# A decoder step on one core: TensorE's side work as single products between the big products, in place of runs at the start of a block

## The chip, the cores and the metric

One core of one Trainium2 chip runs the whole kernel. The metric is device time in microseconds (us): the median of three runs. "Product" below means one matrix product or one transpose issued to TensorE (PE in the profile). A product of plain fp32 operands shows as two matmul instructions in the profile, a transpose and an fp32r product as one.

## The reference, cut to what matters

One layer of a hybrid decoder, on 256 prompt rows and 8 x 4 sample rows, all in fp32:

```
proj = x @ w_in                                   # 2048 -> 11280 columns
gB, gC, h, q, k, v, z, b, a, m_a, m_b = split(proj)
y_a  = (gB * conv3(gC * h)) @ w_a_out
q, k, v = silu(conv4(q|k|v)); q, k l2-normalised; beta = sigmoid(b); g = -exp(a_log) * softplus(a + dt_bias)
# per head, per chunk of 64 rows:
M = strict_lower(beta k k^T * decay);  T = inverse(I + M)
u = T (v beta);  w = T (k beta exp(gcum));  attn = q k^T * decay
v_new = u - w S;  o = q' S + attn v_new;  S = S * exp(g_last) + k'^T v_new
y_b  = (gated RMSNorm(o) * silu(z)) @ w_b_out
x = LN(ALPHA x + (sig(m_a) y_a + sig(m_b) y_b) @ w_o)
x = LN(ALPHA x + relu(x @ w_up)^2 @ w_down)
```

The outputs are y for prompt and sample, and the new conv and delta-rule states.

## The kernel before, in words

**Big products.** Every weight matrix is cut into blocks of 512 KB: 4 slices of 128 rows by 256 columns. 496 blocks are worked off in one list. A weight is split into a high part (ScalarE, `split_hi`, L179) and a low part (VectorE, `split_lo`, L186 by the helper of L140), both fp32r, and so are the activations. `matmuls(i)` issues 24 products for block i: for each 128 x 128 weight tile high x high, high x low, low x high (L206 to L208), each with 288 moving columns (290 in the up projection), accumulated in a PSUM tile `acc`. These 11,904 products are called big products here.

**The order.** The main loop (L1371) writes the program by hand, block after block: `split_hi(i + 3)`, one step of the side work, `split_lo(i + 3)`, the evacuations of `acc` that are due in this block (`due`, L1397), `matmuls(i)`, and the load of block i + 7. Each engine executes its own instructions in just this order; between engines there are semaphores. Four raw, high and low weight buffers rotate, so `split_hi(i + 3)` waits until block i - 1 has been multiplied.

**Side work** is all else that TensorE does, and what ScalarE, VectorE and GpSimd do with it. It is written as generators. `side()` runs `gates()` and then `gdn(G)` for two groups of four heads; a `yield` ends a step, and the main loop takes one step per block. `aux` holds a second generator, `sample()` of the current group or `states()`, with one step per block too. So all products of a step stand as one run ahead of block i's big products, and the step's other instructions follow the run at once. The products that matter below:

- L1030 and L1031: k k^T and q k^T for four chunks of four heads. Stationary 128 x 64, moving 64 columns, results on PSUM partitions 0 to 63 or 64 to 127 by the parity of the head. 32 products, one run per G.
- `pairs` (L1080, products on L1084): block inverse by doubling, for s = 8, 16, 32, two calls each. Eight pairs of 64 x 64 products, one on the lower and one on the upper half of the rows and columns. Six calls per G.
- `states_of` (products on L1072): initial states of the sample rows. Stationary 128 x 64, moving 128 columns, 16 products in a run; two calls per G, each right behind a `pairs` run.
- L1251: state update k'^T v_new, contraction over 64 rows, four products per chunk, four chunks per G; then L1254, two products over the full array.
- Products and transposes over the full array: L958, L973, L980, L1219 (transposes of k, q, v), L1139 to L1142, L1157, L1165, L1172, L1176, L1183 (sample rows), L1203 (sample state), L1231, L1243 (recurrence), L1291, L1298, L1316, and L608 and L628 in the last phase.

`fill` (L159) is a separate list for the first three blocks: x's 16 tiles are transposed by `x_tile(k)`, three transposes each (the third, L799, over 32 rows only), one tile behind each three big products. `hist_tiles()` transposes nine small tiles ahead of block 4. `gtile()` gives the PSUM tiles for side work, four in rotation.

## Time and profile before

| | before |
|---|---|
| median of three runs (lowest, highest) | 1706.18 us (1704.86, 1707.64) |
| span of the profiled execution | 1703.4 us |
| TensorE matmul busy | 1688.5 us, 13,063 instructions |
| VectorE, ScalarE, GpSimd busy | 1007.2, 734.1, 133.8 us |
| first big product starts, last one ends (us from the span's start) | 9.44, 1688.2 |
| side work between them | 90 runs, 1,105 matmul instructions |

The profile gives the profiled execution's time only as its span, 1703.4 us, which is 2.8 us under the median of the runs. In rows of the timeline the columns are start (us), length (us), engine, source line, operation, tile written <- tiles read, rows x columns of the stationary tile, shape of the moving operand, number of instructions merged. A matmul's length runs to the modelled end of its pipeline, so lengths of neighbours overlap; what a product costs is read from the starts. In rows of the stretches the columns are the stretch, its length, busy us and instruction count of PE, PE's weight loads, DVE, ACT and POOL, then the granted clock, the DMA share and GB/s.

### The profile page before, as it was taken

What the parts mean: (1) busy time and instruction counts of PE and PEld (TensorE: products, weight loads), DVE (VectorE), ACT (ScalarE), POOL (GpSimd) and SP (SyncE); (2) the same over time, 40 slices, a digit from 0 to 9 for tenths busy, and PEclk for the clock granted to TensorE, in tenths of its full rate; (3) what the DMA queues carried; (4) which work ended last, traced back from release to release, by engine and by line L of the source; (5) the groups of instructions that cost most, each with busy time, mean ns of one, the idle gap of its engine ahead of it and who ended that gap; (6) DMA issues with size and microseconds to landing.
All of it is one profiled execution on the core that took longest, in us unless ns stands there. A gap on an engine that the chain in (4) does not pass through costs nothing.

```text
span 1703.4 us, 31106 instructions
## 1 busy us (share of the span) xinstructions
PE 1688.5 (99%) x13063; PEld 1668.7 (98%) x13063; DVE 1007.2 (59%) x1296; ACT 734.1 (43%) x1067; POOL 133.8 (8%) x223
## 2 busy tenths in 40 slices
PE   9999999999999999999999999999999999999997
PEld 7999999999999999999999999999999999999997
DVE  5577876758544444456778844566445654466565
ACT  4675626333543333334445533444334433344442
POOL 2232412023300000000010000000000000000000
PEclk9999999999999999999999999999999999999999
DMA  8464456435555555555565555555555555555552
GB/s 244 140 194 139 123 175 200 150 115 180 162 170 169 166 162 170 163 164 165 158 190 174 165 170 161 164 170 162 167 168 161 163 171 162 164 167 164 162 162 80
DMA packets 275097, 279.18 MB, mean 164 GB/s; under 512 B 13131, under 2 KB 270092, under 8 KB 274952
## 3 DMA queue, kind: packets, MB, share of 16 engines
q1 hardware_dynamic: 270414, 265.95, 51.3%
q0 software_dynamic: 4256, 11.12, 2.3%
q8 instruction: 102, 1.67, 0.4%
q14 instruction: 37, 0.30, 0.1%
q10 hardware_dynamic: 288, 0.13, 0.0%
HBM read 269.68 MB, written 7.48 MB: 163 GB/s over the span
## 4 chain that ended last, share of the span: by engine, by line
PE 98%; DVE 1%; DMA 0%; POOL 0%; issue 0%; SPq 0%; ACT 0%; POOLq 0%; ACTq 0%
PE acc L206 31%; PE acc L208 31%; PE acc L207 31%; PE g L1084 1%; DMA xr<-in_x_prompt_dram 0%; PE g L1072 0%; PE g L1231 0%; PE g L1251 0%; PE g L831 0%; DVE w L143 0%; PE g L1254 0%; PE g L1203 0%; PE g L1243 0%; PE g L608 0%; PE g L798 0%; PE g L958 0%
## 5 line engine op out<-in xcount | busy, mean ns | idle before, releaser
L140 DVE TENSOR_TENSOR lo<-raw,hi 128x1024 fp32r<-128x1024 f32 (+2 forms) x502 | 614.0, 1226 | 556.2 <-ACT hi L179 553.7
L179 ACT CAST hi<-raw 128x1024 fp32r<-128x1024 f32 (+1 forms) x498 | 517.6, 1041 | 765.0 <-PE acc L207 707.7
L206 PE MATMUL acc<-xh,hi 128*128 128x288 f32 x1408 | 422.9, 300 | 0.0
L208 PE MATMUL acc<-xh,lo 128*128 128x288 f32 x1408 | 416.7, 296 | 0.0
L207 PE MATMUL acc<-xl,hi 128*128 128x288 f32 x1408 | 416.5, 296 | 0.0
L206 PE MATMUL acc<-dh,hi 128*128 128x290 f32 x1024 | 303.9, 297 | 0.0
L207 PE MATMUL acc<-dl,hi 128*128 128x290 f32 x1024 | 303.3, 296 | 0.0
L208 PE MATMUL acc<-dh,lo 128*128 128x290 f32 x1024 | 302.7, 296 | 0.0
L206 PE MATMUL acc<-hh,hi 128*128 128x288 f32 x1024 | 302.3, 295 | 0.0
L208 PE MATMUL acc<-hh,lo 128*128 128x288 f32 x1024 | 302.3, 295 | 0.0
L207 PE MATMUL acc<-hl,hi 128*128 128x288 f32 x1024 | 302.3, 295 | 0.0
L206 PEld LDWEIGHTS acc<-xh,hi 128*128 128x128 f32 x1408 | 265.4, 189 | 2.6 <-issue 0.7
L207 PEld LDWEIGHTS acc<-xl,hi 128*128 128x128 f32 x1408 | 265.8, 189 | 0.5
L208 PEld LDWEIGHTS acc<-xh,lo 128*128 128x128 f32 x1408 | 265.6, 189 | 0.0
L206 PEld LDWEIGHTS acc<-dh,hi 128*128 128x128 f32 x1024 | 193.6, 189 | 0.1
L208 PEld LDWEIGHTS acc<-dh,lo 128*128 128x128 f32 x1024 | 193.3, 189 | 0.0
L207 PEld LDWEIGHTS acc<-dl,hi 128*128 128x128 f32 x1024 | 193.3, 189 | 0.1
L207 PEld LDWEIGHTS acc<-hl,hi 128*128 128x128 f32 x1024 | 192.5, 188 | 0.0
L208 PEld LDWEIGHTS acc<-hh,lo 128*128 128x128 f32 x1024 | 192.3, 188 | 0.0
L206 PEld LDWEIGHTS acc<-hh,hi 128*128 128x128 f32 x1024 | 192.1, 188 | 0.0
L207 PE MATMUL acc<-ml,hi 128*128 128x288 f32 x256 | 75.6, 295 | 0.0
L208 PE MATMUL acc<-mh,lo 128*128 128x288 f32 x256 | 75.6, 295 | 0.0
(404 smaller groups left out, 1620.0 us busy)
## 6 DMA issues: line engine op xcount, KB each, us to landing
raw<-in_w_in_dram SPq DMA_DIRECT2D x176, 512.0 KB, 3.5
raw<-in_w_up_dram SPq DMA_DIRECT2D x128, 512.0 KB, 3.9
raw<-in_w_down_dram SPq DMA_DIRECT2D x128, 512.0 KB, 3.7
raw<-in_w_o_dram SPq DMA_DIRECT2D x32, 512.0 KB, 3.7
raw<-in_w_a_out_dram SPq DMA_DIRECT2D x16, 512.0 KB, 3.7
raw<-in_w_b_out_dram SPq DMA_DIRECT2D x16, 512.0 KB, 3.6
S<-in_state_gdn_dram POOLq DMA_DIRECT2D x8, 512.0 KB, 7.8
out_dram<-S POOLq DMA_DIRECT2D x8, 512.0 KB, 4.9
```

The source lines that it names most:

```text
L140: dve.tensor_tensor(out=out, in0=a, in1=b, op=op)
L179: act.copy(his[i][:, k:k + step], raw[i][:, k:k + step])
L206: pe.matmul(o, wh, xh_, start=st, stop=False)
L207: pe.matmul(o, wh, xl_, start=False, stop=False)
L208: pe.matmul(o, wl, xh_, start=False, stop=en)
L1084: pe.matmul(out[r, q * 64:q * 64 + 64], a[r, q, :], b[r, q, :], start=True, stop=True)
```

## The change

`fill` is replaced by a list `live` of generators. `slot()` advances the first of them to its next `yield 1`, that is by one product (or one pair), and is called behind every single big product; what is still left at the end of a block is run out there. The side generators get a `yield 1` behind each product, so a step still takes one block but its products stand one behind each big product; its first product still stands ahead of the block. An ordinary `yield` still ends the step. `steps()` takes one step of `sgen` and one of `aux`, product by product. Since a step is now written while `matmuls(i)` is, its ScalarE and VectorE instructions stand behind `split_lo(i + 3)` and the evacuations of block i, no longer ahead of them. In the k k^T part the loops are turned round, so that a pair on both parities is one unit.

```diff
-    fill = []
+    live = []
+
+    def slot():
+        while live:
+            if next(live[0], None):
+                return
+            live.pop(0)
...
                 pe.matmul(o, wh, xh_, start=st, stop=False)
+                slot()
                 pe.matmul(o, wh, xl_, start=False, stop=False)
+                slot()
                 pe.matmul(o, wl, xh_, start=False, stop=en)
-                if fill:
-                    fill.pop(0)()
+                slot()
+        while live:
+            slot()
...
         for c in range(4):
-            for hh in range(4):
-                par = hh % 2
-                q = (c * 2 + hh // 2) * 64
-                ks_ = kq[:, hh, c, par, :]
-                pe.matmul(kkp[rows[par], q:q + 64], ks_, ks_, start=True, stop=True)
-                pe.matmul(kqp[rows[par], q:q + 64], ks_, kq[:, hh, c, 1 - par, :], start=True, stop=True)
+            for p in range(2):
+                q = (c * 2 + p) * 64
+                for out, other in ((kkp, 0), (kqp, 1)):
+                    for par in range(2):
+                        hh = 2 * p + par
+                        pe.matmul(out[rows[par], q:q + 64], kq[:, hh, c, par, :], kq[:, hh, c, par ^ other, :],
+                                  start=True, stop=True)
+                    yield 1
...
                 for par in range(2):
                     pe.matmul(o[rows[par]], kqm[:, par, 64 * b:64 * b + 64], S0[:, 2 * p + par, b, :],
                               start=(b == 0), stop=(b == 7))
+                yield 1
...
                 for par in range(2):
                     r = rows[par]
                     pe.matmul(out[r, q * 64:q * 64 + 64], a[r, q, :], b[r, q, :], start=True, stop=True)
+                yield 1
...
-            pairs(px, nM, Tm)
+            yield from pairs(px, nM, Tm)
...
                 pe.matmul(p3[hh % 2][:, hh // 2, :], kdec[r, c, hh // 2, :], v[r, c, hh // 2, :],
                           start=True, stop=True)
+                if hh % 2:
+                    yield 1
             for p in range(2):
                 pe.matmul(p4[:, p * P:(p + 1) * P], aT[:, 2 * c + p, :], v[:, c, p, :], start=True, stop=True)
+                yield 1
...
+    def step(g, over):
+        r = next(g, 0)
+        while r:
+            yield 1
+            r = next(g, 0)
+        if r == 0:
+            over()
+
+    def steps():
+        if sgen:
+            yield from step(sgen[0], sgen.clear)
+        if aux:
+            yield from step(aux[0], lambda: aux.pop(0))
...
-        if i > 3 and sgen:
-            if i == mark["merge"]:
-                for _ in sgen:
-                    pass
-                sgen = None
-            else:
-                next(sgen, None)
-                if aux and next(aux[0], aux) is aux:
-                    aux.pop(0)
+        if i == 3:
+            live.append(hist_tiles())
+        if i > 3:
+            if i < mark["merge"]:
+                live.append(steps())
+                slot()
...
         for f in due.pop(i, ()):
-            f()
+            g = f()
+            if g is not None:
+                live.append(g)
```

All other side products get a `yield 1` in the same way: one behind each transpose of `x_tile` but the last, of `hist_tiles` (which now runs inside block 3, behind 14 empty slots), of `gates`, of k, q and v, of the outputs and states, of `turned` and so of `out_tiles` and `collect` in the last phase, and between the sample products. The 32 products of L831 stay two runs of 16, L422 and L466 stay as they are, and so does everything behind the last big product.

On TensorE, the first `pairs` of G = 0 before (L206 to L208 are big products; `xt` and `gl` hold the operands of the doubling, `g` is the side work's PSUM tile):

```order
L206 MATMUL acc_1716<-xh,hi_1702 128x288
L207 MATMUL acc_1716<-xl,hi_1702 128x288
L208 MATMUL acc_1716<-xh,lo_1704 128x288
L1084 MATMUL g_1869<-xt_1538,gl_1537 64x64 x16
L206 MATMUL acc_1899<-xh,hi_1743 128x288
L207 MATMUL acc_1899<-xl,hi_1743 128x288
L208 MATMUL acc_1899<-xh,lo_1765 128x288
```

The same place in the changed kernel, where L212, L214 and L216 are the big products and L1119 is `pairs`:

```order
L216 MATMUL acc_1716<-xh,lo_1704 128x288
L1119 MATMUL g_1869<-xt_1567,gl_1566 64x64 x2
L212 MATMUL acc_1884<-xh,hi_1743 128x288
L1119 MATMUL g_1869<-xt_1567,gl_1566 64x64 x2
L214 MATMUL acc_1884<-xl,hi_1743 128x288
L1119 MATMUL g_1869<-xt_1567,gl_1566 64x64 x2
L216 MATMUL acc_1884<-xh,lo_1747 128x288
L1119 MATMUL g_1869<-xt_1567,gl_1566 64x64 x2
```

One run of 16 small products has become eight pairs with a big product between each two; `states_of` and the k k^T part look alike.

On TensorE, the state update of the first chunk of G = 0 before (L1251 contracts over 64 rows; L1254 and the sample product L1165 use the full array):

```order
L208 MATMUL acc_2369<-xh,lo_2209 128x288
L1251 MATMUL g_2398<-v_2253,kdec_1130 128x128
L1251 MATMUL g_2399<-v_2253,kdec_1130 128x128
L1251 MATMUL g_2398<-v_2253,kdec_1130 128x128
L1251 MATMUL g_2399<-v_2253,kdec_1130 128x128
L1254 MATMUL g_2400<-v_2253,aT_1123 128x128 x2
L1165 MATMUL g_2412<-b_1120 128x128
L206 MATMUL acc_2369<-xh,hi_2247 128x288
```

The same place in the changed kernel (L1297, L1302 and L1205 are those products):

```order
L216 MATMUL acc_2369<-xh,lo_2194 128x288
L1297 MATMUL g_2398<-v_2253,kdec_1130 128x128
L1297 MATMUL g_2399<-v_2253,kdec_1130 128x128
L212 MATMUL acc_2369<-xh,hi_2247 128x288
L1297 MATMUL g_2398<-v_2253,kdec_1130 128x128
L1297 MATMUL g_2399<-v_2253,kdec_1130 128x128
L214 MATMUL acc_2369<-xl,hi_2247 128x288
L1302 MATMUL g_2400<-v_2253,aT_1123 128x128
L216 MATMUL acc_2369<-xh,lo_2239 128x288
L1302 MATMUL g_2400<-v_2253,aT_1123 128x128
L212 MATMUL acc_2369<-xh,hi_2247 128x288
L1205 MATMUL g_2428<-b_1120 128x128
```

The four products over 64 rows stand as two pairs, and the full-array products one by one.

On VectorE, the state update of a later chunk of G = 0 before (`lo` is a `split_lo`, `w` a convolution of an evacuation, `E` the delta-rule state, `S` the sample state):

```order
L143 SCALAR_TENSOR_TENSOR w_2558<-w_2558,hw 128x312 x3
L140 TENSOR_TENSOR lo_2600<-raw_2454,hi_2595 128x1024
L143 SCALAR_TENSOR_TENSOR w_2602<-w_2602,hw 128x312 x3
L143 SCALAR_TENSOR_TENSOR E_2314<-E_2314,gexp,g_2640 128x128
L143 SCALAR_TENSOR_TENSOR E_2314<-E_2314,gexp,g_2641 128x128
L143 SCALAR_TENSOR_TENSOR E_2314<-E_2314,gexp,g_2640 128x128
L143 SCALAR_TENSOR_TENSOR E_2314<-E_2314,gexp,g_2641 128x128
L140 TENSOR_TENSOR xt_2315<-xt_2315,g_2642 128x256
```

The same place in the changed kernel:

```order
L140 TENSOR_TENSOR lo_2600<-raw_2454,hi_2595 128x1024
L143 SCALAR_TENSOR_TENSOR w_2602<-w_2602,hw 128x312 x3
L140 TENSOR_TENSOR lo_2645<-raw_2489,hi_2638 128x1024
L143 SCALAR_TENSOR_TENSOR E_2314<-E_2314,gexp,g_2640 128x128
L143 SCALAR_TENSOR_TENSOR E_2314<-E_2314,gexp,g_2641 128x128
L143 SCALAR_TENSOR_TENSOR E_2314<-E_2314,gexp,g_2640 128x128
L143 SCALAR_TENSOR_TENSOR E_2314<-E_2314,gexp,g_2641 128x128
L140 TENSOR_TENSOR xt_2315<-xt_2315,g_2642 128x256
```

One more `split_lo`, that of the block itself, now stands ahead of the step's own instructions.

## The prediction

> **What bounds the kernel now.** I read the page first: engines' busy shares, the slices, the chain of waits.

> ```profile
> PE 1688.5 (99%) x13063; PEld 1668.7 (98%) x13063; DVE 1007.2 (59%) x1296; ACT 734.1 (43%) x1067; POOL 133.8 (8%) x223
> PEclk9999999999999999999999999999999999999999
> PE 98%; DVE 1%; DMA 0%; POOL 0%; issue 0%; SPq 0%; ACT 0%; POOLq 0%; ACTq 0%
> PE acc L206 31%; PE acc L208 31%; PE acc L207 31%; PE g L1084 1%; DMA xr<-in_x_prompt_dram 0%; PE g L1072 0%; PE g L1231 0%; PE g L1251 0%; PE g L831 0%; DVE w L143 0%; PE g L1254 0%; PE g L1203 0%; PE g L1243 0%; PE g L608 0%; PE g L798 0%; PE g L958 0%
> ```

> TensorE is the chain: 98% of it, of which 93% big products. So a nanosecond of TensorE is a nanosecond of the kernel, and every row below is read for one thing: the distance between starts of big products with side work between them. Then the stretch view, for the price of a big product.

> ```profile
> 800.00:1600.00 800.00, 800.00 (x6003) 799.79 (x6003) 470.88 (x523) 325.98 (x410) 6.09 (x12) 1.00 0.55 167
> ```

> 800 us / 6003 = 0.133 us from one big product to the next; 11,904 of them make 1586 of the 1703.4 us. The rest is the start (9.4), the end (15.2) and about 93 us of side work in between. Only this last part is touched.

> **Full-array products: alone or in a run, the same.** The timeline has both: one lone transpose, and eight in a run.

> ```profile
> 275.48 0.29 PE L208 MATMUL acc<-xh,lo 128*128 128x288 f32 x1
> 275.61 0.27 PE L1298 MATMUL g<-cf,osm 128*128 128x128 f32 x1
> 275.64 0.38 PE L206 MATMUL acc<-xh,hi 128*128 128x288 f32 x1
> 275.86 0.30 PE L207 MATMUL acc<-xl,hi 128*128 128x288 f32 x1
> ...
> 92.70 0.29 PE L208 MATMUL acc<-xh,lo 128*128 128x288 f32 x1
> 92.83 1.04 PE L958 MATMUL g<-cf,kq 128*128 128x128 f32 x8
> 93.62 0.38 PE L206 MATMUL acc<-xh,hi 128*128 128x288 f32 x1
> 93.84 0.30 PE L207 MATMUL acc<-xl,hi 128*128 128x288 f32 x1
> ```

> Always from the big product ahead to the second one behind, less two big products (0.27): the lone one costs 275.86 - 275.48 - 0.27 = 0.11, the run 93.84 - 92.70 - 0.27 = 0.87, or 0.109 each. L1298's place is just what the change makes of every full-array product, so some 300 of them get nothing, and lose at most 0.002 to 0.005 each: 0 to +1 us. The bounds from below, if a lone load hides, stand with the rivals. [...]

> x's tiles keep their products, and each keeps its one 32-row product between full-array ones (16 before, 16 after), so 0. L831, L422, L466 and the end are not touched. No queue of SP is reordered, and no DMA but the state stores on POOL moves; they wait in no path of TensorE.

> **Products on part of the array: each pair pays what a run paid once.** Here the rows speak differently. `pairs`, first run:

> ```profile
> 149.28 0.29 PE L208 MATMUL acc<-xh,lo 128*128 128x288 f32 x1
> 149.50 1.15 PE L1084 MATMUL g<-xt,gl 64*64 64x64 f32 x32
> 150.58 0.40 PE L206 MATMUL acc<-xh,hi 128*128 128x288 f32 x1
> 150.82 0.29 PE L207 MATMUL acc<-xl,hi 128*128 128x288 f32 x1
> ```

> Two edges: the first small product starts 0.22 behind the last big one, not 0.13, and behind the run the first big one needs 0.24 to the next. The full-array run above starts 0.13 behind its big product. The run costs 1.54 - 0.27 = 1.27 for 32 instructions, 16 steps of two halves that overlap. The price of a step within a run, from k k^T and q k^T:

> ```profile
> 121.06 0.29 PE L208 MATMUL acc<-xh,lo 128*128 128x288 f32 x1
> 121.28 0.34 PE L1030 MATMUL g<-kq 128*64 128x64 f32 x4
> ...
> 121.56 0.34 PE L1030 MATMUL g<-kq 128*64 128x64 f32 x4
> ...
> 123.08 0.34 PE L1031 MATMUL g<-kq 128*64 128x64 f32 x4
> 123.34 0.40 PE L206 MATMUL acc<-xh,hi 128*128 128x288 f32 x1
> 123.58 0.30 PE L207 MATMUL acc<-xl,hi 128*128 128x288 f32 x1
> ```

> From 121.56 to 123.08 are 13 rows of four instructions, two steps each: 1.52 / 26 = 0.0585 a step. What the change puts behind a big product is a pair, two steps. So it costs a run less 14 steps: 1.27 - 14 x 0.0585 = 0.45, where it cost 1.27 / 8 = 0.16 in the run. Of the 0.45 nearly all is edge.

> - `pairs`: 6 calls x 2 groups G x 8 pairs = 96 x 0.45 = 43.2; before 12 x 1.27 = 15.2. **+28.0**.
> - k k^T: a run costs 2.52 - 0.27 = 2.25 for 32 steps; a pair 2.25 - 30 x 0.0585 = 0.50. 2 x 16 x 0.50 = 16.0 for 4.5. **+11.5**.

> `states_of`, behind a run of `pairs`:

> ```profile
> 153.73 0.29 PE L208 MATMUL acc<-xh,lo 128*128 128x288 f32 x1
> 153.95 1.15 PE L1084 MATMUL g<-U,xt 64*64 64x64 f32 x32
> 155.03 1.97 PE L1072 MATMUL g<-S,b 128*64 128x128 f32 x32
> 156.93 0.40 PE L206 MATMUL acc<-xh,hi 128*128 128x288 f32 x1
> 157.17 0.30 PE L207 MATMUL acc<-xl,hi 128*128 128x288 f32 x1
> ```

> From 155.03 to 156.93 are 1.90 for 16 steps of 128 columns, 0.109 each as in L958's row: two steps and the way out are 1.90 - 14 x 0.109 = 0.37. With the way in (0.22) and the slow first big product (0.24), less 0.27, a pair costs 0.56. 4 calls x 8 x 0.56 = 17.9 for 4 x 1.90 = 7.6. **+10.3**.

> ```profile
> 235.66 0.29 PE L208 MATMUL acc<-xh,lo 128*128 128x288 f32 x1
> 235.89 0.71 PE L1251 MATMUL g<-v,kdec 64*128 64x128 f32 x8
> 236.53 0.71 PE L1254 MATMUL g<-v,aT 128*128 128x128 f32 x4
> 237.00 0.38 PE L206 MATMUL acc<-xh,hi 128*128 128x288 f32 x1
> 237.21 0.29 PE L207 MATMUL acc<-xl,hi 128*128 128x288 f32 x1
> ```

> L1251, four steps: way in 0.23, 0.64 to L1254, of which two steps (0.22) go: 0.23 + 0.42 + 0.24 - 0.27 = 0.62 a pair. Before: 1.55 - 0.27 less L1254's four at 0.11 = 0.84. 16 x 0.62 = 9.9 for 8 x 0.84 = 6.7. **+3.2**. The three 32-row transposes of L841, once a run and now alone, I take at one more edge each for two of them, as in `pairs`: **+0.5**.

> Sum for TensorE: 28.0 + 11.5 + 10.3 + 3.2 + 0.5 = +53.5. Nothing covers it, since TensorE is the chain. Below, the edge could cost nothing when only a pair stands there (then each pair costs its two steps: 0, or a gain; rival D); above, it could be dearer than in a run, for which no row speaks.

> **Waits.** The one large wait of TensorE in the middle, and the stretch around it:

> ```profile
> PE g L1203 <- DVE E L143: 3.0, 1, 3.0
> 180.00:215.00 35.00, 33.80 (x265) 32.78 (x263) 32.22 (x44) 22.31 (x46) 16.11 (x18) 1.00 0.40 121
> ```

> L1203's second product waits 3.0 us for a PSUM tile that the state update on VectorE reads. There VectorE is busy 32.2 of 35 us, so it is behind. The change gives this wait six more big products ahead of it (6 x 0.133 = 0.8), but puts one more `split_lo` ahead of the update, and one lasts 1.2 us as in the list of groups:

> ```profile
> L140 DVE TENSOR_TENSOR lo<-raw,hi 128x1024 fp32r<-128x1024 f32 (+2 forms) x502 | 614.0, 1226 | 556.2 <-ACT hi L179 553.7
> ```

> So +0.4 there. Elsewhere each step's VectorE and ScalarE work now stands behind a `split_lo` (1.2) and often an evacuation, while its TensorE result comes up to 16 products later; in return blocks with pairs last 3.6 us longer (8 x 0.45). Between 0 (all in the slack that a step has until the next block) and some 12 us (ten steps each late by 1.2); I take +1, near the low end, since in the doublings, where the products come latest, the blocks grow most.

> Full: 1703.4 + 53.5 + 1 = 1757.9 for the span; the median of the runs lies 2.8 above the span, so **1761 us**. A measurement tells from no change what is over 0.2%, 3.4 us (the three runs of before lie 2.8 apart).

> **The rivals.**

> - **B, the clock falls in the doublings.** A block with `pairs` and `states_of` lasts 24 x 0.133 + 8 x 0.45 + 8 x 0.56 = 11.3 us, with a big product only each 0.6 to 0.7 us. The end of the profile shows the granted clock fall while the last products had hardly ended:

> ```profile
> 1694.00:1696.00 2.00, 1.81 (x8) 0.78 (x6) 1.67 (x5) 1.76 (x4) 0.15 (x1) 1.00 0.29 109
> 1696.00:1698.00 2.00, 0.00 (x0) 0.00 (x0) 0.71 (x1) 1.53 (x3) 1.92 (x2) 0.60 0.99 386
> 12.00:20.00 8.00, 8.00 (x31) 6.77 (x32) 4.08 (x8) 3.67 (x8) 0.52 (x4) 1.00 1.08 289
> 20.00:30.00 10.00, 10.00 (x64) 8.33 (x64) 4.56 (x10) 4.15 (x11) 0.00 (x0) 1.00 0.86 210
> ```

>   So thin work does not hold the clock. For it: the pairs leave the array idle over half the time. Against: from 20 to 30 us x's tiles stand between big products, 64 instructions in 10 us, and it holds. The price: 8.0 / 31 = 0.258 us an instruction at the start against 0.156 from 20 us on, in much the same mix, a factor 1.65 (the recorded clock is 1.00 in both, so it tells nothing of the start). The doublings last 4 x 6.8 + 2 x 11.3 = 50 us per G; 2 x 50 x 0.65 = +65 at most, half of it if the clock falls half way: 1793 to 1826. [...]
> - **C, lone loads hide.** If a lone full-array product's load ran under the big product, at most its 0.11 would go: 300 x 0.11 = 33, half of it 16: 1728 to 1745. The row of L1298 is against it.
> - **D, faster: no edge for a pair.** If a big product of another shape could stream while the pair is loaded, the edges (0.09 in, 0.11 behind, and the way out) would not add up. It decides at 0.16 a pair, the price in the run; at that, and with L1203's wait gone, 1706.2 - 3.0 = 1703. Against it are the edges of all 23 runs of such products. [...]
> - **E, a new wait.** TensorE waits at ten or more steps for late VectorE and ScalarE work: 1761 + 15 to + 39: 1776 to 1800.

> **How the numbers follow.** The sum (A, 1748 to 1775) 0.76, B 0.12, C 0.05, E 0.05, D 0.02. Range 1742 to 1800: it holds A, E, B's low end and C's high end, and leaves out some 0.15. Faster is D, 0.02; the same 0.01; slower 0.97.

> **What would show it.** L1119 (was L1084) in 96 pieces of four instructions, the first 0.22 behind a big product (0.33 from the start of one that follows a pair), and two such big products 0.58 apart, not 0.133; the same with 0.7 for L1106; the stretches of full-array side work as long as before; the clock at full. It is wrong if a pair between two big products costs 0.2 or less, if big products double their distance in the doublings, or if waits of TensorE for VectorE or ScalarE sum to over 10 us.

## The result, and the profile after

| | before | after |
|---|---|---|
| median of four runs (lowest, highest), same chip | 1706.79 us (1704.86, 1707.64) | 1773.85 us (1770.60, 1774.89) |
| ratio, 95% interval | | 1.0393 (1.0379 to 1.0408) |
| span of the profiled execution | 1703.4 us | 1773.1 us |
| between big products, beyond 0.1332 us for each of them | 93.0 us | 162.5 us |

The change costs 67 us, 3.9%. The last row is summed from the starts of the big products in the two timelines; it grows by 69.5 us, and the span by 69.7. So all of the loss lies between big products, and the start and the end of the program have no part in it.

The page of after: busy time, granted clock by slices, the chain of waits.

```profile
PE 1753.6 (99%) x13063; PEld 1693.8 (96%) x13063; DVE 1007.3 (57%) x1296; ACT 735.4 (41%) x1067; POOL 135.7 (8%) x223
PEclk9999899999999999999999999999999999999999
PE 96%; DVE 1%; issue 1%; ACT 0%; DMA 0%; SPq 0%; POOLq 0%; POOL 0%; ACTq 0%; DVEq 0%
```

TensorE has the same 13,063 instructions and is busy 65.1 us longer. VectorE and ScalarE do the same work in the same time. One slice has a granted clock under 0.9; before had none. The stretch that priced a big product reads as before:

```profile
800.00:1600.00 800.00, 800.00 (x6004) 799.68 (x6003) 467.76 (x518) 324.06 (x401) 6.00 (x11) 1.00 0.55 167
```

Here nothing has changed; the rows of the account below lie in the first 500 us but for single products of the last phase, which cost what they did. Timeline of TensorE in after, a block with `pairs` (L1119), then one with `states_of` (L1106); L212, L214 and L216 are the big products:

```profile
155.85 0.33 PE L1119 MATMUL g<-xt,gl 64*64 64x64 f32 x4
156.11 0.40 PE L214 MATMUL acc<-xl,hi 128*128 128x288 f32 x1
156.44 0.33 PE L1119 MATMUL g<-xt,gl 64*64 64x64 f32 x4
156.70 0.40 PE L216 MATMUL acc<-xh,lo 128*128 128x288 f32 x1
...
166.51 0.40 PE L214 MATMUL acc<-xl,hi 128*128 128x288 f32 x1
166.84 0.44 PE L1106 MATMUL g<-S,b 128*64 128x128 f32 x4
167.21 0.40 PE L216 MATMUL acc<-xh,lo 128*128 128x288 f32 x1
```

Big products with a pair between them stand 156.70 - 156.11 = 0.59 us apart, with a pair of `states_of` 167.21 - 166.51 = 0.70. A pair begins 0.33 behind the start of its big product, and the next big product 0.26 (0.37) behind the pair.

The waits of TensorE in after (line that waits, what for, us in total, times, longest):

```profile
PE g L1288 <- DVE v L143: 4.7, 2, 3.0
PE g L1297 <- DVE v L140: 2.3, 1, 2.3
PE g L1246 <- DVE E L143: 0.8, 2, 0.5
```

Before, the one large wait was L1203 for E, 3.0. That is 0.8 now (L1246), and two others have come, at the recurrence's L1288 and at L1297, each for VectorE. Stretches of after, with the granted clock as third column from the end:

```profile
180.93:184.34 3.41, 3.41 (x31) 2.28 (x30) 1.23 (x1) 0.43 (x1) 0.00 (x0) 1.00 0.14 24
184.34:187.76 3.42, 3.42 (x16) 1.75 (x15) 1.44 (x2) 0.00 (x0) 0.00 (x0) 0.50 0.38 129
...
194.58:198.00 3.42, 3.42 (x18) 2.75 (x17) 0.32 (x1) 2.24 (x7) 0.00 (x0) 0.50 0.00 0
198.00:201.41 3.41, 3.41 (x32) 2.15 (x29) 2.45 (x4) 0.69 (x3) 1.23 (x3) 1.00 0.36 95
...
242.37:245.78 3.41, 1.13 (x9) 0.90 (x7) 3.38 (x4) 0.25 (x1) 3.27 (x5) 1.00 0.41 140
245.78:249.20 3.42, 3.38 (x16) 2.68 (x16) 3.35 (x6) 2.14 (x6) 0.00 (x0) 0.50 0.23 44
```

The clock is granted by half from 184.34 to 198.00 (in the middle of the doublings of G = 0), from 245.78 to 252.61 (behind L1297's wait) and from 454.00 to 457.41 (behind a wait of L1288). In the first of these, 16 to 18 instructions go through in a stretch where there are 31 or 32 on both sides of it.

**The account of the +69.5 us**, from the two timelines:

| | us |
|---|---|
| edges of products on part of the array | +53.2 |
| half clock: 5.4 at 184.34, 3.1 at 245.78, 1.5 at 454.00 | +10.0 |
| waits for VectorE, 9.5 against some 4.0 | +5.5 |
| full-array products alone (113 ns each, 109 in a run) | +0.6 |
| sum | +69.3 |

### The profile page after: what moved, and what is told of

The parts are those of the page before. It is cut to its first block, busy times and chain, and to the rows that moved or that the text cites. A ratio compares the mean times of both kernels' runs of the same rounds, so it can differ in the third digit from the quotient of the medians.

```text
span 1773.1 us, 31116 instructions
## 1 busy us (share of the span) xinstructions
PE 1753.6 (99%) x13063; PEld 1693.8 (96%) x13063; DVE 1007.3 (57%) x1296; ACT 735.4 (41%) x1067; POOL 135.7 (8%) x223
## 3 DMA queue, kind: packets, MB, share of 16 engines
q8 instruction: 102, 1.67, 0.4%
## 4 chain that ended last, share of the span: by engine, by line
PE 96%; DVE 1%; issue 1%; ACT 0%; DMA 0%; SPq 0%; POOLq 0%; POOL 0%; ACTq 0%; DVEq 0%
PE acc L214 30%; PE acc L212 30%; PE acc L216 30%; PE g L1119 1%; PE g L1106 1%; PE g L1063 0%; DMA xr<-in_x_prompt_dram 0%; DVE w L143 0%; PE g L813 0%; ACT hi L185 0%; PE g L1297 0%; DVE lo L140 0%; PE g L852 0%; PE g L1246 0%; PE g L619 0%
## 5 line engine op out<-in xcount | busy, mean ns | idle before, releaser
L140 DVE TENSOR_TENSOR lo<-raw,hi 128x1024 fp32r<-128x1024 f32 (+2 forms) x502 | 611.1, 1220 | 639.8 <-ACT hi L185 625.5
L212 PE MATMUL acc<-xh,hi 128*128 128x288 f32 x1408 | 432.9, 307 | 0.0
L214 PE MATMUL acc<-xl,hi 128*128 128x288 f32 x1408 | 431.5, 306 | 0.0
L216 PE MATMUL acc<-xh,lo 128*128 128x288 f32 x1408 | 428.8, 305 | 0.0
L212 PE MATMUL acc<-dh,hi 128*128 128x290 f32 x1024 | 303.9, 297 | 0.0
L214 PE MATMUL acc<-hl,hi 128*128 128x288 f32 x1024 | 303.6, 296 | 0.0
L214 PE MATMUL acc<-dl,hi 128*128 128x290 f32 x1024 | 303.3, 296 | 0.0
L216 PE MATMUL acc<-hh,lo 128*128 128x288 f32 x1024 | 303.0, 296 | 0.0
L216 PE MATMUL acc<-dh,lo 128*128 128x290 f32 x1024 | 302.7, 296 | 0.0
L212 PE MATMUL acc<-hh,hi 128*128 128x288 f32 x1024 | 302.3, 295 | 0.0
L212 PEld LDWEIGHTS acc<-xh,hi 128*128 128x128 f32 x1408 | 267.4, 190 | 7.4 <-issue 2.8
L214 PEld LDWEIGHTS acc<-xl,hi 128*128 128x128 f32 x1408 | 267.8, 190 | 6.1 <-issue 1.9
L216 PEld LDWEIGHTS acc<-xh,lo 128*128 128x128 f32 x1408 | 267.5, 190 | 5.1 <-issue 2.5
L212 PEld LDWEIGHTS acc<-dh,hi 128*128 128x128 f32 x1024 | 193.6, 189 | 0.1
L216 PEld LDWEIGHTS acc<-dh,lo 128*128 128x128 f32 x1024 | 193.3, 189 | 0.0
L214 PEld LDWEIGHTS acc<-dl,hi 128*128 128x128 f32 x1024 | 193.3, 189 | 0.1
L214 PEld LDWEIGHTS acc<-hl,hi 128*128 128x128 f32 x1024 | 192.4, 188 | 0.0
L216 PEld LDWEIGHTS acc<-hh,lo 128*128 128x128 f32 x1024 | 192.3, 188 | 0.0
L212 PEld LDWEIGHTS acc<-hh,hi 128*128 128x128 f32 x1024 | 192.1, 188 | 0.0
L214 PE MATMUL acc<-ml,hi 128*128 128x288 f32 x256 | 75.6, 295 | 0.0
L216 PE MATMUL acc<-mh,lo 128*128 128x288 f32 x256 | 75.6, 295 | 0.0
```

What stands on the lines that cost most here:

```text
L140: dve.tensor_tensor(out=out, in0=a, in1=b, op=op)
L212: pe.matmul(o, wh, xh_, start=st, stop=False)
L214: pe.matmul(o, wh, xl_, start=False, stop=False)
L216: pe.matmul(o, wl, xh_, start=False, stop=en)
```

## The experiments

Each ratio is to before on the same chip; before had 1705.72 us there (e1, e2, e4, e5) or 1706.81 us (e6 to e9). Small differences between experiments of the two groups are best read from each one's distance to its own before.

**e1: the part-array products as runs again.** In after, the `yield 1` is taken out in k k^T, `states_of`, `pairs`, the state update and L841's loop; all full-array products stay single.

```diff
                     pe.matmul(out[r, q * 64:q * 64 + 64], a[r, q, :], b[r, q, :], start=True, stop=True)
-                yield 1
...
-            yield from pairs(px, nM, Tm)
+            pairs(px, nM, Tm)
```

> The changed kernel with the products on part of the array (k k^T, pairs, states_of, L1251, L841) put back into runs; all full-array products stay single behind big products. Theory (each pair on part of the array pays an edge, full-array products pay nothing alone): +0.5 us for the singles and up to +5 us of waits against the kernel before, no fall of the clock in the doublings: 1707 to 1713 us. Rival (the single placement as such costs, or the later VectorE work): it keeps most of the +67 us, over 1740. Rival (lone loads hide): under 1700.

1720.58 us (1719.77 to 1722.20), ratio 1.0082 (1.0067 to 1.0097). This takes 53.3 us off after's median, which the sum of the edges had as 53.5: the edges are the loss's main part, and rival D is out. But 14.9 us more than before are left where 1 to 7 were expected. Its waits:

```profile
PE g L1284 <- DVE v L143: 5.1, 2, 3.4
PE g L1242 <- DVE E L143: 4.0, 2, 2.9
PE g L1293 <- DVE v L140: 2.3, 1, 2.3
```

L1284, L1242 and L1293 are after's L1288, L1246 and L1297. By the starts of the big products, waits now come to 14.9 us, and there are three half-clock stretches of 3.41 us, which cost 4.1. So with the edges gone, the waits for VectorE got larger: blocks are short again, and the step's VectorE work comes late. Since e1 has 5.9 us less of half clock than after (4.1 for 10.0) and 5.4 us more of waits (14.9 for 9.5), two changes that nearly cancel, part of the agreement between 53.3 and 53.5 is luck; the edges alone are then some 53 us.

**e2: the full-array products as runs again,** the part-array pairs kept: after without the `yield 1` in `gates`, `gdn`, `sample` and `states` behind full-array products.

```diff
                 pe.transpose(kv[:, hh, :], kq[:, hh, c].rearrange("p s x -> p (s x)"), ident)
-                yield 1
```

> The changed kernel with the full-array products of gates, gdn, sample and states put back into runs; only the products on part of the array (and x, the small history tiles and the last phase) stay single. Theory: all of the +53 us of edges and most of the +10 us of half clock stay: 1765 to 1775 us. Rival (the singles of the full array carry the loss): under 1730.

1767.34 us (1760.87 to 1773.59), ratio 1.0355 (1.0320 to 1.0390). As expected the loss stays; rival C (single loads hide) would have made these runs 16 to 33 us slower than after, and it is out. Its runs lie 12.7 us apart, with mean granted clocks from 0.988 to 0.995, so the 6.5 us to after are not to be read more closely.

**e4: the order alone.** Before, with no product moved within a block's run; only the side step is taken behind `split_lo(i + 3)` and the due evacuations, as it is in after.

```diff
             else:
-                next(sgen, None)
-                if aux and next(aux[0], aux) is aux:
-                    aux.pop(0)
+                pass
...
         for f in due.pop(i, ()):
             f()
+        if i > 3 and sgen:
+            next(sgen, None)
+            if aux and next(aux[0], aux) is aux:
+                aux.pop(0)
```

> The kernel before with one thing moved: the step of the side work is written behind split_lo(i + 3) and the evacuations of block i, as in the changed kernel; TensorE's order stays in runs. It takes the waits by themselves. Theory (waits of the changed kernel, 9.5 us against 4 before, come from VectorE's order): +3 to +7 us, 1710 to 1714, with TensorE's waits for VectorE at 7 to 11 us in the profile. Rival (they come from products that are issued later in the block): within 2 us of before, 1705 to 1709.

1723.47 us (1722.56 to 1724.50), ratio 1.0098 (1.0083 to 1.0113). The direction is right, the size is not: +17.8 us for the order alone. The waits name what is late:

```profile
PE g L1203 <- DVE E L143: 6.0, 2, 4.4
PE g L1243 <- DVE v L143: 5.3, 3, 3.4
PE g L980 <- POOL vmh L976: 1.6, 1, 1.6
PE g L1172 <- DVE b L1166: 1.2, 1, 1.2
```

L1203's wait has doubled from 3.0, and the three others are not among before's. The granted clock fell by half for 6.8 us at 220.0 and for 3.4 us at 257.5 and 400.9, behind these waits.

**e8 and e9: the order taken back by another way.** In after (e8) and in e1 (e9), `split_lo(i + AHEAD)`, which is `split_lo(i + 3)`, is moved behind `matmuls(i)`, so that the step's VectorE work no longer stands behind it.

```diff
-        split_lo(i + AHEAD)
         for f in due.pop(i, ()):
...
         matmuls(i)
+        split_lo(i + AHEAD)
```

> The changed kernel with split_lo(i + 3) written behind block i's products, so that a step's VectorE work stands ahead of it again (the evacuations stay ahead). Theory (waits come from the split_lo put ahead of the step): waits of TensorE for VectorE from 9.5 to 3 to 6 us, and the falls of the clock behind them go: -5 to -10 us, 1764 to 1769. Rival (the evacuations or the late products make the waits): over 1771.

e8: 1761.79 us (1760.17 to 1769.86), ratio 1.0333 (1.0312 to 1.0354), 12.1 us under after, more than the 5 to 10 that were expected. TensorE's waits are 5.3 us where after had 9.5, and one half-clock stretch of 3.4 us is left. Of the three waits in after's rows above, L1288's and L1297's are down to 1.0 and 0.2, and L1246's has grown from 0.8; one of 1.1 for GpSimd has come (L1010):

```profile
PE g L1246 <- DVE E L143: 2.2, 1, 2.2
PE g L1010 <- POOL vmh L1006: 1.1, 1, 1.1
```

> The kernel of the first experiment (products on part of the array in runs, the rest single) with the same move of split_lo(i + 3). Theory: most of its +15 us goes, 1706 to 1712 us. If lone full-array products also spared waits, it would come under the kernel before, 1700 to 1704. Rival (as above): over 1716.

e9: 1710.48 us (1707.89 to 1712.63), ratio 1.0019 (1.0011 to 1.0028). With the edges and the place of `split_lo` undone, and every full-array product still single, before's time is nearly back (the evacuations still stand ahead of the step). Each against its own before, after has +67.1 us, e1 +14.9 and e9 +3.7. So the loss splits into the edges (after to e1) 52.2, the place of `split_lo` (e1 to e9) 11.2, and 3.7 for all that is left. That the three make the whole follows from how they are formed; that the first agrees with the timelines' 53.2 does not. What the 3.7 are is open. They include the single products, so no gain from those shows.

**e5: four pairs behind each big product,** after with a `yield 1` at every fourth pair of `pairs` and `states_of` and at every fourth of k k^T: 40 groups in place of 160.

```diff
-                yield 1
+                if q % 4 == 3:
+                    yield 1
```

> The changed kernel with the pairs of k k^T, pairs and states_of in groups of four behind one big product, so 40 groups in place of 160; L1251 as in the changed kernel. Theory (the cost is the number of edges): a group of four costs 0.45 + 6 x 0.0585 = 0.80 us (states_of 0.575 + 6 x 0.109 = 1.23); 24 x 0.80 + 8 x 0.81 + 8 x 1.23 = 35.5 in place of 76.8, so -41 us, and -5 us since the clock holds in the doublings: 1725 to 1735. Rival (the clock or waits carry the loss, not the edges): over 1750.

1728.71 us (1727.51 to 1729.67), ratio 1.0126 (1.0109 to 1.0143): 45.1 us under after. The timeline of e5 (L1120 is `pairs`):

```profile
156.16 0.40 PE L212 MATMUL acc<-xh,hi 128*128 128x288 f32 x1
156.49 0.68 PE L1120 MATMUL g<-U,xt 64*64 64x64 f32 x16
157.10 0.40 PE L214 MATMUL acc<-xl,hi 128*128 128x288 f32 x1
```

The group of 16 instructions costs 157.10 - 156.16 = 0.94, the pair of 4 cost 0.59. The edges are the same (0.33 in, a slow big product behind): less one big product it is 0.81, and 0.45 and six more steps of 0.0585 make 0.80. That leaves 120 edges fewer; at 0.34 each (0.454 less two steps of 0.0585) 41 us, and 45.1 were measured. The clock, which holds through the doublings in e5 (after lost 5.4 us there) and falls later for 6.83 us at 220.9 and at 405.2, is the likely rest; this run does not separate it. The cost follows the number of edges, not the number of products.

**e7: does thin work make the clock fall?** After with a second `yield 1` in `states_of`, so that its pairs stand behind every second big product.

```diff
                               start=(b == 0), stop=(b == 7))
                 yield 1
+                yield 1
```

> The changed kernel with states_of's pairs behind every second big product in place of every one. Theory (the clock fell at 184 us because a window of 3.4 us held too little work; edges as before): no fall of the clock in the doublings, -5 us: 1766 to 1770 us. Rival (the clock falls for the number of edges, or the profile's 13.7 us at half clock cost nothing): 1772 to 1776.

1772.04 us (1770.53 to 1786.80), ratio 1.0406 (1.0366 to 1.0447). The window of 3.4 us is as long as after's shortest stretch at half clock, 454.00 to 457.41. The result is not the theory's 1766 to 1770, but it refutes nothing either: the half-clock stretch at 184.34 went, but two of 3.41 us came in blocks with `pairs`, at 177.5 and 378.9, and three behind waits, at 242.4, 279.9 and 450.6.

**e6: one edge fewer in before.** The prediction's edges speak for a change that nobody made: the third transpose of each x tile (L799) works on 32 rows, between full-array products. In before, all 128 rows are transposed; the rows beyond the 32 are zeroed once, and the added columns are not read.

```diff
+    for i in range(4):
+        dve.memset(xr[i][32:64, 2, :], 0.0)
+        dve.memset(xr[i][64:128, 2, :], 0.0)
...
-        pe.transpose(g[:, NP_:NT], xr[i][0:NS, 2, kk * P:(kk + 1) * P], ident[0:NS, 0:NS])
+        pe.transpose(g[:, NP_:NP_ + P], xr[i][:, 2, kk * P:(kk + 1) * P], ident)
```

> The kernel before with the third transpose of each x tile over all 128 rows (rows 32 to 127 cleared to zero first, results not used) in place of 32 rows. Theory (the edge comes from a change of the part of the array in use, not from how little a product does): x's tiles of blocks 1 and 2, 0.59 us each between big products, fall to 0.33, 8 x 0.26 = -2.1 us, and the eight at half clock ahead of them save up to as much again: 1702 to 1705 us, though the product itself is larger. Rival (the price is that of the product): same or slower, 1706 or more.

1700.77 us (1699.88 to 1702.09), ratio 0.9967 (0.9954 to 0.9979): a small gain, but faster than both kernels, and under the 1702 to 1705 that were expected. An x tile in before, then in e6 (L798/L801 are the first two transposes, L799/L802 the third):

```profile
21.45 0.30 PE L208 MATMUL acc<-xh,lo 128*128 128x288 f32 x1
21.58 0.38 PE L798 MATMUL g<-cf,xr 128*128 128x128 f32 x2
21.89 0.24 PE L799 MATMUL g<-cf,xr 32*128 32x32 f32 x1
22.07 0.40 PE L206 MATMUL acc<-xh,hi 128*128 128x288 f32 x1
22.30 0.29 PE L207 MATMUL acc<-xl,hi 128*128 128x288 f32 x1
```

```profile
16.41 0.29 PE L208 MATMUL acc<-xh,lo 128*128 128x288 f32 x1
16.54 0.38 PE L801 MATMUL g<-cf,xr 128*128 128x128 f32 x2
16.76 0.27 PE L802 MATMUL g<-cf,xr 128*128 128x128 f32 x1
16.79 0.38 PE L206 MATMUL acc<-xh,hi 128*128 128x288 f32 x1
17.00 0.30 PE L207 MATMUL acc<-xl,hi 128*128 128x288 f32 x1
```

From the big product ahead to the second one behind: 0.85 in before, 0.59 in e6. A transpose with four times the rows is 0.26 cheaper, since it has no edge. Both transposes are plain fp32 among fp32r products, so the edge is not that of a change of type. Twelve tiles stand between big products, 3.1 us in all; by the starts of the big products the tiles cost 10.2 us before and 4.9 in e6. The other 2.1 are the start: from 12 to 20 us e6 has twice the instructions of before's 31. Rows of e6, then of e9:

```profile
12.00:20.00 8.00, 7.92 (x63) 7.67 (x61) 4.46 (x10) 4.67 (x12) 1.16 (x5) 1.00 1.08 288
...
12.00:18.51 6.51, 6.51 (x26) 5.56 (x26) 3.05 (x7) 3.29 (x8) 0.55 (x4) 0.50 1.08 283
```

So TensorE has its full rate earlier there, and the clock's record goes with it. In e6's trace the record opens with the full clock at 9.96 us, in before's at 20.48; the 1.00 that rows show ahead of that is no record. e9's record opens earlier, and it shows the half clock from 8.27 to 18.51 us, where instructions go through at before's rate (26 in 6.51 us, 31 in 8.00). So part of e6's gain is that the clock was granted some 10 us earlier. All five runs of e6 lie below all 15 of before; whether the full-array transposes brought the grant forward is not settled.

## Why the prediction was right, and where it was not

1773.85 against 1761, inside the range; slower, as forecast.

- **The edges, +53.5:** measured +53.2 in the timelines and 52.2 to 53.3 by e1. Each pair of `pairs` 454 ns for 0.45 (93 of them at full clock), of `states_of` 578 for 0.56, of k k^T 460 for 0.50, a pair of L1297 0.62 by its median for 0.62. That a pair pays what a run pays less its missing steps was right within a tenth in every row. The sum came closer than its terms: k k^T is +10.2 for +11.5, and `pairs` (+28.3) and `states_of` (+10.9) make up for most of it. Big products stand 0.59 and 0.70 us apart, as "what would show it" had it (0.58, 0.7).
- **Full-array products, 0 to +1:** +0.6 in the timeline, 113 ns for 109.
- **Waits, +1: too small.** +5.5 us of waits, and 4.6 us of half clock behind them. L1203's wait shrank from 3.0 to 0.8, where the step had it 0.4 longer; in the same block L1297 now waits 2.3 us ahead of it. What the step missed is the recurrence: its products wait for `v`, one after the other, and each chunk's VectorE work now stands behind a `split_lo` and an evacuation. The timeline of TensorE, then of VectorE ahead of this wait (`w<-w,hwa` belongs to an evacuation):

```profile
281.83 0.29 PE L216 MATMUL acc<-xh,lo 128*128 128x288 f32 x1
283.81 0.49 PE L1288 MATMUL g<-v,U 128*128 128x128 f32 x2 [1.69 <-DVE v L143]
284.06 0.38 PE L212 MATMUL acc<-xh,hi 128*128 128x288 f32 x1
```

```profile
279.05 1.23 DVE L140 TENSOR_TENSOR lo<-raw,hi 128x1024 fp32r<-128x1024 f32 x1 [1.04 <-ACT hi L185]
...
282.03 1.10 DVE L143 SCALAR_TENSOR_TENSOR w<-w,hwa,w 128x304 f32<-128x304 f32 x2
283.05 1.45 DVE L143 SCALAR_TENSOR_TENSOR v<-g,gpt,v 64x128 f32<-64x128 f32 x4
```

  The step held that waits would be small "since in the doublings, where the products come latest, the blocks grow most". The recurrence has no pairs but L1297's, so its blocks do not grow, and there the order costs in full. e4 shows how much that is where no block grows at all: its four rows of waits come to 14.1 us where before had 3.0, about the upper bound of 12, and with the half clock behind them it is 17.8 us slower. For L1297's wait the prediction's own row of 180 to 215 us (VectorE busy 32.2 of 35 us) was the place to see it: there VectorE has little room to make up for a late start. L1288's two large waits stand, by the count of big products, at 247 and 387 us of before, for which the prediction shows no row; VectorE is busy 7.4 of 10 us there (240 to 250) and 10.1 of 11 (385 to 396).
- **Rival B, the clock, 0.12:** it came true in part, at the place that it named: 184.34 to 198.00, 5.4 us, not the 32 to 65 that it was priced at. Its factor of 1.65 was right, for 13.65 us there held what takes 8.25 at the full clock; its extent was not, since most of the 50 us of doublings per G kept the clock. Under A it was counted as nothing, and that is the largest term missed: all half-clock stretches together 10.0.
- **Rivals C, D and E:** C and D are refuted by e2, e9 and e1. E's mechanism was there at some six places and cost 5.5 us, or 10.1 with the half clock behind the waits, below its 15.
- **The sum:** the span was forecast at 1757.9 and is 1773.1, 15.2 more: clock 10.0, waits 4.5, singles 0.6, edges -0.3, and 0.4 unaccounted. The 2.8 us from span to median were 0.75 here, since the profiled run of after was the slowest of its four. So the result lies 1 us under the top of A's own range (1748 to 1775) although A had the clock at full: there the width of the range covered what the mechanism left out, and that part is luck. The mark set for the waits was over 10; they came to 9.5.

## What to carry to other kernels

On this kernel a product on part of the array costs 0.34 us at its borders with full-array work, and 0.06 to 0.11 us by itself: keep such products together, or give them the full array with zeros where that is cheap (e6). Spreading full-array products singly cost 0.6 us here and showed no gain. Before side work is moved behind another engine's bulk work, look at what that engine does in that stretch: behind each block's `split_lo` of 1.2 us the side steps cost 11 to 12 us in all (e9, e8), and behind the evacuations as well 17.8 (e4).

## What the runs showed of the hardware that was not expected

**The windows ahead of the falls hold work.** Rows of e6, then of before, where the clock held, then of e1:

```profile
207.93:211.34 3.41, 1.41 (x10) 1.36 (x11) 3.34 (x10) 0.54 (x2) 0.76 (x1) 1.00 0.55 159
211.34:214.75 3.41, 3.41 (x17) 3.41 (x16) 2.22 (x2) 0.00 (x0) 2.01 (x2) 0.50 0.25 71
```

```profile
215.03:218.45 3.42, 1.66 (x11) 1.62 (x12) 3.38 (x10) 0.54 (x2) 1.01 (x1) 1.00 0.50 153
```

```profile
217.64:221.06 3.42, 0.54 (x4) 0.43 (x4) 3.38 (x9) 0.54 (x2) 0.00 (x0) 1.00 0.58 162
221.06:224.47 3.41, 3.41 (x17) 3.41 (x16) 1.26 (x3) 0.00 (x0) 2.77 (x2) 0.50 0.49 150
```

(The grid of before is counted back from its fall at 1696.42.) With TensorE busy 1.41 of 3.41 us the clock fell in e6; with 1.66, ten of the eleven being big products, it held in before. In after, ahead of 454.00, it fell with 1.66 too, four of the twelve being big products:

```profile
450.58:454.00 3.42, 1.66 (x12) 1.48 (x13) 3.31 (x9) 0.19 (x1) 0.00 (x0) 1.00 0.34 117
```

So it is not the profile's busy time alone that decides. What does for the windows with pairs is open: the one ahead of 184.34 has 31 instructions, 6 of them big products, like others that held, and e7 did not settle it. A window at half clock mostly costs 1.2 to 1.6 us (in after 5.4 for four, 3.1 for two and 1.5 for one, in e1 4.1 for three). So a wait can cost a second time: L1297's 2.3 us left the window from 242.37 to 245.78 with TensorE busy for 1.13 us, and the two windows at half clock behind it cost 3.1. The runs of before beside the experiments go the same way: with a mean granted clock of 0.998 the span is 1703.2 to 1703.6 us, with 0.991 it is 1706.1 to 1707.1, and in between 1703.9 to 1705.5; a good part of before's scatter goes with the clock. The mean is a rough measure, since it counts the start at half only where the record reaches back to it.

**VectorE slows beside GpSimd.** In after, VectorE and GpSimd ahead of L1297's wait, and in e4 three of the same instructions with GpSimd at rest:

```profile
240.70 4.73 DVE L143 SCALAR_TENSOR_TENSOR w<-w,hw 128x312 f32<-128x312 f32 x3
240.82 4.27 POOL L1233 TENSOR_TENSOR vm<-v,cf 128x1024 fp32r<-128x1024 f32 x2
```

```profile
217.47 1.69 DVE L143 SCALAR_TENSOR_TENSOR w<-w,hw 128x312 f32<-128x312 f32 x3
```

Three convolution steps take 4.73 us beside GpSimd's work and 1.69 without, and `v`, for which L1297 waits 2.3 us, stands behind them. The trace of after has more of it. The same instruction took 0.53 to 0.55 us all 32 times that GpSimd was idle. Nine overlap a TENSOR_TENSOR of GpSimd: the three that started ahead of it took 0.54 us, and the six that started while it ran took 1.2 to 2.1 and ended 0.34 us behind its end, every one. So in these rows VectorE's instruction is held until GpSimd's has ended; how much of the 2.3 us would go without it is open, since no run took it away.
